# An SSD mixer whose small matmuls get a fixed order, with a projection unit between them, and weight low parts made by an accumulating DMA

## The chip, the cores and the metric

The kernel runs on one NeuronCore of a Trainium2 chip. The metric is the device time of one execution in microseconds (us). A core has the engines PE (TensorE, the matrix engine), DVE (VectorE), ACT (ScalarE), POOL (GpSimd) and SP (SyncE, which here only issues DMAs); each works through its own instructions in their fixed order and waits on semaphores for the others. DMAs are issued by SP, ACT or POOL and run beside the engines.

## What is computed

One inference step of a two-layer trunk for 512 prompt tokens and 8 x 8 sample tokens, 576 columns in all. Each layer is a half-step SwiGLU FFN, a mixer and another half-step FFN, with RMSNorm ahead of each. The mixer of layer 0, the one that matters here, is a Mamba-2 SSD mixer:

```python
def ssd_mixer(h, ssm0, conv0, w_in, conv_w, conv_b, dt_bias, a_log, d_skip, norm_g, w_out):
    proj = h @ w_in                                   # 1024 -> 2048 (z) + 4096 (x, B, C) + 32 (dt)
    z, xbc, dt_raw = jnp.split(proj, [D_INNER, D_INNER + CONV_DIM], axis=-1)
    xbc, conv_new = causal_dwconv(xbc, conv0, conv_w, conv_b)
    xs, Bm, Cm = jnp.split(jax.nn.silu(xbc), [D_INNER, D_INNER + SSD_GROUPS * D_STATE], axis=-1)
    dt = jax.nn.softplus((dt_raw + dt_bias).astype(f32))
    y, ssm_new = ssd_scan(xs, dt, A, Bm, Cm, ssm0)    # chunks of 128, 32 heads of 64, 8 groups, 128 states
    y = (y + d_skip * xs).reshape(bsz, l, D_INNER) * jax.nn.silu(z)
    ...                                               # RMSNorm within each of the 8 groups
    return y @ w_out, ssm_new, conv_new
```

Inside a chunk the scan multiplies a masked decay matrix exp(a_l - a_s) by C·B and applies it to x·dt; the states at the chunks' ends are chained, read out through C, and returned. All matrices are float32.

## The kernel before, in words

The activations lie transposed, 128 channels on the partitions and the 576 tokens along the row. A float32 product is made of three passes with rounded operands: weights and activations are split into a high part (a rounded copy) and a low part (the rest), and high·high, high·low and low·high are added up. A **unit** is one output tile of 128 channels: 8 blocks of 128 rows, three passes, two halves of 288 tokens, 48 matmuls of 128x288 (L339, in `passes`). Its weights come by one SP load of 512 KB into one of two `raw` buffers; `block` cuts them in two, writes the high part on ACT (L317) and the low part by a subtraction (L318), on POOL in this stage, into one of six `wb` buffers (two a unit). An output projection unit (`outproj`) has 2 or 4 blocks, so 12 or 24 matmuls.

The SSD stage has 48 units of w_in: 16 tiles of x (ct 0 to 15), 8 of B (16 to 23), 8 of C (24 to 31), 16 of z. `conv_in` runs a unit of x, B or C and the convolution behind it: three products with the norm's scale into `ext` (L637 to L639), ACT's first tap into `cacc` (L645) and three DVE taps (L647). The state of the convolution is loaded and transposed ahead of that, as four `crow` tiles of eight transposes each (L654, L657), through one buffer.

The 32 heads form 8 groups g of 4 heads, and each group two pairs j of two heads; p = 2g + j counts pairs. `group` makes, from B and C of a group, B with tokens on the partitions (`bnat`), C·B (`cbs`) and a block form of the sample tokens' B (`bblk`). `pair` does the scan of two heads: it transposes the old states (`nat` to `h0t`) and x, forms x·dt (`xdt`) and x·decay (`xw`, `xs`, `xd`), loads the decay sums `m` by SP (L800), masks them on POOL (L808 to L810), takes exponentials on ACT (L813), multiplies by `cbs` on DVE (L814, L815), and runs the small matmuls for states (L851), read-out (L864), the diagonal part (L871, L873) and the state update (L840). `spread` and four transposes prepare the decay numbers of all heads once. `gnorm` norms a group when its successor runs (`rnat`, L184, and `rbcast`, L218).

PSUM has eight banks: two `acc2` tiles of two banks in this stage (a unit's output each), and four `misc` banks for all small results.

The order of the instructions on each engine comes from the framework's scheduler, which lists them by a simulated time line (`TileContext(nc, schedule_with_timeline_sim=True)`) unless two of them were named by `tc.keep_in_program_order`, which then stay in the order of the code. Before, only the read-out and diagonal products of a pair are named so:

```python
for n, c in enumerate((3, 2, 1)):
    t = PE.matmul(out=pu[:, (c - 1) * P:c * P], lhsT=ht[:, c - 1], rhs=ctl[:, c * P:(c + 1) * P], start=True, stop=True)
    if n:
        pin(t)
```

All other small matmuls fall where the scheduler puts them, between the big ones of the units.

Of the kernel before, what the change touches and what calls it, by code (L numbers as in the profile page):

```python
# [8 lines left out]
F32 = mybir.dt.float32  # L9
# [40 lines left out]
def trunk(ctx, tc, x_prompt, x_sample, state_ssm, state_conv, state_pool,  # L50
# [127 lines left out]
    def rnat(accs, width):  # L178
        pt = misc()
        for c, (t0, n) in enumerate(BLOCKS):  # L180
            for h in range(0, P, 64):
                for i, acc in enumerate(accs):
                    t = t0 + h % n
                    PE.matmul(out=pt[h:h + 64, c:c + 1], lhsT=acc[:, t:t + 64], rhs=ones[:, 0:1], start=i == 0, stop=i == len(accs) - 1)  # L184
        return rstd(pt[:, 0:5], width)
# [28 lines left out]
    def rbcast(r):  # L214
        pt, pt2 = misc(), misc()
        for c, (t0, n) in enumerate(BLOCKS):
            o = pt[:, t0:t0 + n] if c < 4 else pt2[:, 0:n]
            PE.transpose(out=o, in_=r[0:n, c:c + 1].broadcast_to([n, P]), identity=ident[0:n, 0:n])  # L218
# [92 lines left out]
    def block(src, eng=None, pool=None):  # L311
# [6 lines left out]
        (eng or V).tensor_tensor(out=lo, in0=src, in1=hi.bitcast(F32), op=ALU.subtract)  # L318
# [15 lines left out]
    def passes(pd, w, acts, first, last):  # L334
        for h in range(2):
            n = 0
            for (wh, wl), (ah, al) in zip(w, acts):
                for lt, a in ((wh, ah), (wh, al), (wl, ah)):
                    PE.matmul(out=pd[:, h, 0:HALF], lhsT=lt, rhs=a[:, h * HALF:(h + 1) * HALF],  # L339
                              start=first and n == 0, stop=last and n == 3 * len(acts) - 1)  # L340
                    n += 1

    def mm(pt, w, acts):
        kn = len(acts)
        for k in range(0, kn, 4):
            passes(pt, w[k:k + 4], acts[k:k + 4], k == 0, k + 4 >= kn)
# [240 lines left out]
    def ssd(tail):  # L587
# [5 lines left out]
        with ExitStack() as st:  # L593
# [31 lines left out]

            def proj(c0, w=None):
                pt = acc_tile()
                mm(pt, w or unit(win[:, :, c0:c0 + P], G), hs)
                return pt

            def conv_in(ct):
# [4 lines left out]
                V.tensor_copy(out=es[:, :, 0:3], in_=cst[:, ct].rearrange("p (b e) -> p b e", e=3))  # L636
# [5 lines left out]
                V.tensor_copy(out=tails[:, ct, 3:27].rearrange("p (b e) -> p b e", e=3), in_=es[:, :, XST - 3:XST])  # L642
                a = wk.tile([P, XW], F32, name="cacc")
                n = XS0 + NB * XST - 3
                S.activation(out=a[:, 0:n], in_=ext[:, 0:n], func=AF.Identity, scale=cw[:, ct:ct + 1], bias=col("cb", ct))  # L645
                for k in range(1, 4):
                    V.scalar_tensor_tensor(out=a[:, 0:n], in0=ext[:, k:k + n], scalar=cw[:, k * 32 + ct:k * 32 + ct + 1], in1=a[:, 0:n],  # L647
                                           op0=ALU.mult, op1=ALU.add)
                return a
# [51 lines left out]
            pre = {}  # L701
            for ct in (16, 24):
                pre[ct] = conv_in(ct)
# [41 lines left out]
            V.tensor_scalar(out=mh[0:32], in0=mh[0:32], scalar1=hv[0:32, 2:3], scalar2=None, op0=ALU.mult)  # L745
            def spread():
                pt = misc()
                self_ = sel.rearrange("h a b -> h (a b)")
                PE.matmul(out=pt[:, 0:P], lhsT=self_, rhs=rhs.rearrange("h a b -> h (a b)"), start=True, stop=True)
# [21 lines left out]
            pin = tc.keep_in_program_order  # L771

            def stack(pt, src):
                s3 = wk.tile([P, 2, 3, 32], F32, name="s3", bufs=1)
                S.copy(out=s3, in_=src[:, SEQ:T].rearrange("p (q s) -> p q s", q=2).unsqueeze(2).broadcast_to([P, 2, 3, 32]))
                for q in range(2):
                    PE.transpose(out=pt[0:96, q * P:(q + 1) * P], in_=s3[:, q].rearrange("p a s -> p (a s)"), identity=ident)

            def pair(g, j, bt, ctl, bnat, bblk, cbs, xst, yt):
# [5 lines left out]
                h0t = wk.tile([P, NB, P], F32, name="h0t", bufs=1)  # L785
                for q in range(2):
                    pt = misc()
                    for i in range(4):
                        PE.transpose(out=pt[:, i * P:(i + 1) * P], in_=nat[:, 4 * q + i], identity=ident)
                    (V.tensor_copy if q else S.copy)(out=h0t[:, 4 * q:4 * q + 4], in_=pt.rearrange("p (b n) -> p b n", n=P))  # L790
                pq = misc()
                for b in range(NB):
                    r = b % 4 * 32
                    o = SEQ + b // 4 * 32
                    PE.matmul(out=pq[r:r + 32, (2 + b // 4) * P:(3 + b // 4) * P], lhsT=ctl[:, o:o + 32], rhs=h0t[:, b], start=True, stop=True)
                ch = wk.tile([P, 2, P], F32, name="ch", bufs=1)
# [423 lines left out]
```

## Time and profile before

| | us |
|---|---|
| median of three runs | 2357.1 (2356.55 to 2357.26) |
| the profiled execution: its time | 2357.4 |
| the profiled execution: span from first to last instruction | 2355.6 |
| PE busy | 2282.7 (97%) |
| DVE busy | 1874.8 (80%) |
| ACT busy | 1053.1 (45%) |
| POOL busy | 1030.7 (44%) |
| mean granted clock of PE | 0.987 |

PE has two clock levels, 1.2 and 2.4 GHz; the granted clock of a stretch is given as a share of the higher one. The SSD stage lies between about 423 and 1005 us; ahead of it and behind it are FFNs, which the change leaves as they are. A busy PE is not PE at its peak, since matmuls overlap and their ends are modelled: a rate is better read from the distance between the starts. Numbers in round brackets with an x are counts of instructions, in square brackets stands the time that an engine was idle just before, and what ended it.

### The profile page before, as it was taken

To read this page: it belongs to the slowest core of one execution; us is meant where nothing else is said; L and a number is where in the kernel's file an instruction comes from. 1 tells how busy PE (TensorE), PEld (TensorE's weight loads), DVE (VectorE), ACT (ScalarE), POOL (GpSimd) and SP (SyncE) were. 2 spreads that over 40 slices of the span, in tenths; PEclk is the share of its full clock that TensorE was granted. 3 is DMA by queue.
4 is the path that set the end of the run, shared out by engine and by line. 5 is a ranking of instruction groups with operands and counts; after the bars stand their busy time and mean duration, and the time that the engine had idled before them with its cause. 6 is when DMAs were issued, how large, how long until landed. Compare 5 with 4: busy or idle time off the path is not lost.

```text
span 2355.6 us, 43789 instructions
## 1 busy us (share of the span) xinstructions
PE 2282.7 (97%) x17572; PEld 2241.3 (95%) x17572; DVE 1874.8 (80%) x2950; ACT 1053.1 (45%) x1947; POOL 1030.7 (44%) x796
## 2 busy tenths in 40 slices
PE   8999999999999999989999999999999999999998
PEld 7999999988999999979999999999999899999997
DVE  8987778688887786798877799778876859778876
ACT  6444434455554545354444354334444344344433
POOL 4555440344444444155554535555531325555530
PEclk9999999999999999999999999999999999999999
DMA  5223222243443334412232232323222242322221
GB/s 150 90 90 108 81 90 66 62 138 110 134 135 107 118 110 113 116 57 88 90 108 82 89 99 72 108 64 99 90 81 67 67 117 83 108 68 94 90 73 59
DMA packets 272904, 222.23 MB, mean 94 GB/s; under 512 B 8322, under 2 KB 269042, under 8 KB 272701
## 3 DMA queue, kind: packets, MB, share of 16 engines
q1 hardware_dynamic: 269172, 218.04, 30.4%
q8 instruction: 139, 2.28, 0.4%
q10 hardware_dynamic: 3528, 1.39, 0.2%
q14 instruction: 65, 0.52, 0.1%
HBM read 206.46 MB, written 12.94 MB: 93 GB/s over the span
## 4 chain that ended last, share of the span: by engine, by line
PE 60%; DVE 9%; ACT 1%; DMA 1%; issue 1%; DVEq 0%; SPq 0%; ACTq 0%
PE acc L375 29%; PE acc L339 27%; DVE wh L256 1%; PE acc L554 1%; DVE cacc L647 1%; PE acc L479 1%; DVE ws L1102 1%; DVE m L814 0%; DMA rd<-in_pool_w_out 0%; PE misc L871 0%; DVE wb L318 0%; PE misc L851 0%; PE misc L864 0%; DVE glo L256 0%; ACT m L813 0%
## 5 line engine op out<-in xcount | busy, mean ns | idle before, releaser
L375 PE MATMUL acc<-wh,wb 128*128 128x288 f32 x6888 | 920.4, 295 | 4.2 <-DVE fo L380 2.3
L375 PEld LDWEIGHTS acc<-wh,wb 128*128 128x128 f32 x6888 | 916.1, 189 | 5.9 <-ACT wb L317 3.2
L339 PE MATMUL acc<-ghi,wb 128*128 128x288 f32 x2752 | 550.7, 295 | 0.3 <-DVE x L416 0.3
L339 PEld LDWEIGHTS acc<-ghi,wb 128*128 128x128 f32 x2752 | 441.2, 188 | 0.6 <-DVE x L416 0.5
L317 ACT CAST wb<-raw 128x512 fp32r<-128x512 f32 (+1 forms) x440 | 265.7, 607 | 358.8 <-PE acc L339 151.9
L339 PE MATMUL acc<-glo,wb 128*128 128x288 f32 x1376 | 404.2, 295 | 0.0
L339 PE MATMUL acc<-hhi,wb 128*128 128x288 f32 x1824 | 382.8, 300 | 2.3 <-DVE x L414 0.8
L318 POOL TENSOR_TENSOR wb<-raw,wb 128x512 fp32r<-128x512 f32 (+1 forms) x154 | 211.3, 1374 | 339.5 <-ACT wb L317 330.5
L318 DVE TENSOR_TENSOR wb<-ws,wb 128x512 fp32r<-128x512 f32 x328 | 325.8, 1004 | 15.0 <-ACT wb L317 14.9
L318 DVE TENSOR_TENSOR wb<-raw,wb 128x512 fp32r<-128x512 f32 (+1 forms) x286 | 269.3, 956 | 63.8 <-ACT wb L317 63.3
L317 ACT CAST wb<-ws 128x512 fp32r<-128x512 f32 x328 | 202.5, 621 | 241.0 <-PE acc L375 216.8
L339 PEld LDWEIGHTS acc<-hhi,wb 128*128 128x128 f32 x1824 | 297.8, 190 | 5.7 <-issue 1.6
L416 DVE SCALAR_TENSOR_TENSOR x<-acc,x 128x576 f32<-128x576 f32 x160 | 120.6, 754 | 194.8 <-PE acc L339 194.6
L339 PE MATMUL acc<-hlo,wb 128*128 128x288 f32 x912 | 273.4, 300 | 0.0
L356 POOL TENSOR_TENSOR ws<-raw,ws 128x512 f32<-128x512 f32 x82 | 151.9, 1852 | 246.0 <-DVE wb L318 241.0
L339 PEld LDWEIGHTS acc<-glo,wb 128*128 128x128 f32 x1376 | 257.9, 188 | 0.0
L318 POOL TENSOR_TENSOR wb<-rd,wb 128x512 fp32r<-128x512 f32 x128 | 174.8, 1374 | 184.0 <-ACT wb L317 183.8
L317 ACT CAST wb<-rd 128x512 fp32r<-128x512 f32 x196 | 114.0, 592 | 250.1 <-PE acc L339 219.3
L355 POOL TENSOR_TENSOR ws<-raw 128x512 f32<-128x512 f32 x82 | 124.6, 1520 | 160.4 <-DVE wb L318 160.4
L339 PEld LDWEIGHTS acc<-hlo,wb 128*128 128x128 f32 x912 | 173.0, 190 | 0.8 <-issue 0.2
L353 POOL TENSOR_TENSOR ws<-raw 128x512 f32<-128x512 f32 x82 | 128.4, 1566 | 87.5 <-DMA raw<-in_ffn_w_gate 78.4
L354 POOL TENSOR_TENSOR ws<-ws,raw 128x512 f32<-128x512 f32 x82 | 130.3, 1589 | 7.7 <-DVE wb L318 1.5
(329 smaller groups left out, 2897.5 us busy)
## 6 DMA issues: line engine op xcount, KB each, us to landing
raw<-in_ffn_w_gate SPq DMA_DIRECT2D x41, 1024.0 KB
raw<-in_ffn_w_up SPq DMA_DIRECT2D x41, 1024.0 KB
rd<-in_ffn_w_down SPq DMA_DIRECT2D x80, 512.0 KB
raw<-in_ssd_w_in SPq DMA_DIRECT2D x48, 512.0 KB
m<-ad SPq DMA_DIRECT2D x16, 576.0 KB
nat<-in_state_ssm SPq DMA_DIRECT2D x16, 512.0 KB
out<-nat SPq DMA_DIRECT2D x16, 512.0 KB
raw<-in_ssd_w_out SPq DMA_DIRECT2D x24, 256.0 KB
```

Source lines behind the costliest of these rows:

```text
L256: V.scalar_tensor_tensor(out=o, in0=xs, scalar=g, in1=sub, op0=ALU.mult, op1=ALU.subtract)
L317: S.copy(out=hi, in_=src)
L318: (eng or V).tensor_tensor(out=lo, in0=src, in1=hi.bitcast(F32), op=ALU.subtract)
L339: PE.matmul(out=pd[:, h, 0:HALF], lhsT=lt, rhs=a[:, h * HALF:(h + 1) * HALF], start=first and n == 0, stop=last and n == 3 * len(acts) - 1)
L353: G.tensor_tensor(out=s[0], in0=blk[2], in1=blk[3], op=ALU.add)
L354: G.tensor_tensor(out=s[1], in0=s[0], in1=blk[0], op=ALU.subtract)
L355: G.tensor_tensor(out=s[2], in0=blk[2], in1=blk[0], op=ALU.subtract)
L356: G.tensor_tensor(out=s[3], in0=blk[1], in1=s[1], op=ALU.subtract)
L375: PE.matmul(out=pt[:, m, 0:HALF], lhsT=wb[:, j, k], rhs=hh[k, h][:, slot], start=n == 0, stop=n == 11)
L416: V.scalar_tensor_tensor(out=halves(x[:, d]), in0=pt[:, :, 0:HALF], scalar=scale, in1=halves(x[:, d]), op0=ALU.mult, op1=ALU.add)
L479: PE.matmul(out=pd[:, m, 0:HALF], lhsT=w[:, a, 2 * k + m], rhs=b[:, h * HALF:(h + 1) * HALF], start=n == 0, stop=n == 5)
L554: PE.matmul(out=pt[:, m, 0:HALF], lhsT=wb[:, a, k], rhs=hh[k, b][:, slot], start=q == 0 and k == a == b == 0, stop=q == 1 and k == 3 and a ...
```

## The change

Four things change, all in the SSD stage.

**The low parts.** Where POOL subtracted, ACT now writes the negated high part into the low half (L323), and POOL issues a DMA that adds the raw weights to it (L324). PE waits for that DMA. The first two conv units keep the old form, their weights being split earlier.

**The order.** All small matmuls of the stage and the first big one of each unit are named for program order. `pair` becomes a generator that gives up control three times: loads; group A (transposes of the old states and of x); group B (C times old states, chunk states, state update); group C (read-out, diagonal part). In front of A of a first pair stands `group`, behind C of a first pair the norm of the last group. Between any two of them the loop puts a unit: conv 17+g or 25+g before A, conv p+1 between A and B, z between B and C, with four output projection units ahead of z in even groups.

**Where things are done.** Several small copies go from DVE to ACT, the two `m` products become one, `conv_in` is cut into the unit with its scaling and the `taps`, `bnat` and `cbs` come out of one `acc2` tile, the old states out of another, and `cbs` has one buffer for all groups.

**The end.** The first four of the last eight output projection units move up into the last pair.

```diff
-        (eng or V).tensor_tensor(out=lo, in0=src, in1=hi.bitcast(F32), op=ALU.subtract)
+        if eng == "dma":
+            S.activation(out=lo, in_=hi.bitcast(F32), func=AF.Identity, scale=-1.0)
+            G.dma_start(out=lo.bitcast(F32), in_=src, accum_op=ALU.add)
+        else:
+            (eng or V).tensor_tensor(out=lo, in0=src, in1=hi.bitcast(F32), op=ALU.subtract)
...
+                    if held and first and h == n == 0:
+                        tc.keep_in_program_order(t)
...
+                ph, pt, pt2 = acc_tile(), misc(), misc()
+                for b in range(NB):
+                    pin(PE.transpose(out=ph[:, b // 4, b % 4 * P:(b % 4 + 1) * P], in_=nat[:, b], identity=ident))
+                for c, (t0, n) in enumerate(BLOCKS):
+                    o = pt[0:n, c * P:(c + 1) * P] if c < 4 else pt2[0:n, 0:P]
+                    pin(PE.transpose(out=o, in_=xst[:, t0:t0 + n], identity=ident))
+                stack(pt2[:, P:512], xst)
...
+                V.tensor_tensor(out=m, in0=m, in1=cbs.unsqueeze(1).broadcast_to([P, 2, T]), op=ALU.mult)
...
+                pa, pt2 = acc_tile(), misc()
                 for c in range(4):
-                    PE.transpose(out=pt[:, c * P:(c + 1) * P], in_=bt[:, c * P:(c + 1) * P], identity=ident)
-                V.tensor_copy(out=bnat, in_=pt.rearrange("s (c n) -> s c n", n=P))
+                    pin(PE.transpose(out=pa[:, 0, c * P:(c + 1) * P], in_=bt[:, c * P:(c + 1) * P], identity=ident))
+                stack(pt2, bt)
+                for c in range(4):
+                    pin(PE.matmul(out=pa[:, 1, c * P:(c + 1) * P], lhsT=bt[:, c * P:(c + 1) * P], rhs=ctl[:, c * P:(c + 1) * P], start=True, stop=True))
...
+                S.copy(out=bnat, in_=pa[:, 0].rearrange("s (c n) -> s c n", n=P))
+                V.tensor_copy(out=cbs[:, 0:SEQ], in_=pa[:, 1])
...
+                for j in range(2):
+                    p = 2 * g + j
+                    if g < 7:
+                        conv_in((25 if j else 17) + g)
+                    elif j:
+                        zs = zproj(p)
+                    if j == 0:
...
+                        bnat, bblk = group(bt, ctl)
...
+                    work = pair(g, j, bt, ctl, bnat, bblk, x_, yt)
+                    next(work)
+                    if p == 0:
+                        spread()
+                    next(work)
+                    if g < 7 and j == 0:
+                        taps(17 + g)
+                        bc_.append(bt_ctl(g + 1, 0))
...
+                    if p < 15:
+                        conv_in(p + 1)
+                    else:
+                        outproj(10, 4, range(0, 2))
+                    if g and j == 0:
+                        r = rnat([sqacc], 256, True)
+                    next(work)
+                    if p < 15:
+                        taps(p + 1)
+                        x_ = xtile(p + 1)
                     if g % 2 == 0 and g:
                         outproj(max(2 * g - 6, 0), 4 if g > 2 else 2, range(4 * j, 4 * j + 4))
...
+                    if p < 15:
+                        zs = zproj(p)
+                    else:
+                        outproj(10, 4, range(2, 4))
+                    work.send(zs)
```

**What stands where.** PE at the start of the stage, before: the norm's broadcast (`rr`), a run of crow transposes among the big matmuls of the first unit (acc_4805).

```order
L339 MATMUL acc_4805<-hhi,wb 128x288 x2
L339 MATMUL acc_4805<-hlo,wb 128x288
L218 MATMUL misc<-ident,rr 128x128 x4
L218 MATMUL misc<-ident,rr 128x64
L657 MATMUL misc<-ident,crow 128x24 x8
L339 MATMUL acc_4805<-hhi,wb 128x288 x2
L339 MATMUL acc_4805<-hlo,wb 128x288
```

PE at the same place after, from the last matmuls of the dt projection (acc_4726) to the first of that unit:

```order
L347 MATMUL acc_4726<-hlo,wb 128x288
L347 MATMUL acc_4726<-hhi,wb 128x288
L220 MATMUL misc<-ident,rr 128x128 x4
L220 MATMUL misc<-ident,rr 128x64
L673 MATMUL misc<-ident,crow 128x24 x32
L683 MATMUL misc<-ident,vrow 128x3
L347 MATMUL acc_4805<-hhi,wb 128x288
```

The four runs of eight crow transposes, which lay 25 to 30 big matmuls apart, now stand in one run ahead of the unit.

PE where group 1 begins, before: `bnat`'s transposes (L925), the sample tokens' transposes (L777) and C·B (L936) inside one unit (acc_6105).

```order
L840 MATMUL misc<-bblk,xw_5587 128x512
L925 MATMUL misc<-ident,bt 128x128 x4
L339 MATMUL acc_6105<-hhi,wb 128x288 x2
L777 MATMUL misc<-ident,s_5723 96x128 x2
L339 MATMUL acc_6105<-hlo,wb 128x288
L339 MATMUL acc_6105<-hhi,wb 128x288 x2
L339 MATMUL acc_6105<-hlo,wb 128x288
L339 MATMUL acc_6105<-hhi,wb 128x288 x2
L936 MATMUL misc<-ctl,bt 128x128 x4
```

PE at the same place after, from the end of conv unit 18 (acc_5795) to the first matmul of conv unit 3 (acc_5957):

```order
L347 MATMUL acc_5795<-hhi,wb 128x288
L929 MATMUL acc_5868<-ident,bt 128x128 x4
L794 MATMUL misc<-ident,s_5874 96x128 x2
L932 MATMUL acc_5868<-ctl,bt 128x128 x4
L933 MATMUL misc<-ctl,bt 64x64
L811 MATMUL acc_5899<-ident,nat 128x128 x8
L814 MATMUL misc<-ident,xst 128x128 x4
L814 MATMUL misc<-ident,xst 64x128
L794 MATMUL misc<-ident,s_5915 96x128 x2
L347 MATMUL acc_5957<-hhi,wb 128x288
```

`group` and group A stand in one block between two units. acc_5868 (the tile `pa`) is the buffer that acc_5957 takes again, so the last row waits for the copies out of `pa`.

DVE at that place, before, around the copy of `cbs`:

```order
L843 SCALAR_TENSOR_TENSOR nat<-nat,decp,misc 128x128 x3
L926 COPY bnat<-misc 128x512 [waits PE_49]
L969 TENSOR_TENSOR zs<-acc_6026,rb 128x576 [waits DVE_49]
L949 TENSOR_TENSOR sqacc<-sqacc,sq 128x576 [waits Activation_49]
L937 COPY cbs<-misc 128x512 [waits PE_49]
L931 TENSOR_TENSOR bsp<-bns,bsp 32x256 [waits Activation_49]
```

DVE at that place after, from the scaling of unit 18 to the copies out of the two acc tiles:

```order
L649 TENSOR_TENSOR ext<-acc_5795,rb 128x288 [waits PE_49]
L650 TENSOR_TENSOR ext<-acc_5795,rb 128x224
L651 TENSOR_TENSOR ext<-acc_5795,rb 128x8x8
L825 TENSOR_TENSOR xw<-misc,anat 128x512 [waits PE_49]
L828 TENSOR_TENSOR xdt<-misc,anat 128x512
L826 TENSOR_TENSOR xs_5922<-misc,wsn 96x256 [waits PE_49]
L829 TENSOR_TENSOR xd_4653<-misc,anat 64x128
L664 SCALAR_TENSOR_TENSOR cacc<-ext,cw,cacc 128x600 [waits DVE_49,Activation_49,Pool_49]
L935 COPY cbs<-acc_5868 128x512 [waits Activation_49]
L824 COPY h0t<-acc_5899 128x512 [waits Activation_49]
```

The copy of `cbs`, which stood behind work of the pair before, now stands behind the products of the x transposes (L814) and a tap.

## Rows read from the trace of the kernel before

**Rows 1.** The page, part 1: busy us, share of the span, instructions, by engine.

```profile
PE 2282.7 (97%) x17572; PEld 2241.3 (95%) x17572; DVE 1874.8 (80%) x2950; ACT 1053.1 (45%) x1947; POOL 1030.7 (44%) x796
```

**Rows 2.** Windows, whole core: window, us, busy us (x instructions) of PE, PEld, DVE, ACT, POOL, clock, DMA share, GB/s.

```profile
480.00:530.00 50.00, 49.51 (x401) 46.41 (x402) 43.09 (x99) 30.02 (x72) 23.93 (x25) 0.93 0.47 138
...
680.00:730.00 50.00, 47.03 (x379) 44.85 (x378) 39.61 (x85) 26.36 (x55) 21.75 (x20) 0.93 0.37 105
...
830.00:880.00 50.00, 47.69 (x408) 45.77 (x407) 40.55 (x94) 21.41 (x46) 21.27 (x19) 1.00 0.39 113
...
930.00:980.00 50.00, 45.94 (x386) 42.17 (x383) 42.86 (x94) 18.05 (x35) 14.09 (x11) 0.97 0.38 106
```

**Rows 3.** Waits of PE, 423 to 1010: us in total, times, longest.

```profile
PE misc L795 <- DVE h0t L790: 5.1, 3, 2.5
PE misc L749 <- DVE rhs L744: 4.9, 1, 4.9
PE acc L339 <- DVE ext L639: 3.8, 2, 2.3
PE misc L184 <- DVE sqacc L949: 3.0, 1, 3.0
```

**Rows 4.** Timeline of PE: start, us, operation, in brackets the idle time before it.

```profile
477.77 0.58 PE L749 MATMUL misc<-rhs,sel 64*128 64x128 f32 x1 [4.91 <-DVE rhs L744]
```

**Rows 5.** Windows of PE alone: window, us, busy us, granted clock, DMA share, GB/s.

```profile
477.50:487.50 10.00, 9.33 (x47) 0.51 0.63 187
...
541.00:545.00 4.00, 3.86 (x25) 0.62 0.11 31
```

**Rows 6.** Timeline of PE at the end of a run of small matmuls.

```profile
603.96 0.38 PE L339 MATMUL acc<-hlo,wb 128*128 128x288 f32 x1
604.17 0.43 PE L339 MATMUL acc<-hhi,wb 128*128 128x288 f32 x2
604.44 0.29 PE L339 MATMUL acc<-hlo,wb 128*128 128x288 f32 x1
```

**Rows 7.** Timeline of SP's queue: the second and third crow load.

```profile
428.08 4.42 SPq L654 DMA_DIRECT2D crow<-in_state_conv  x2
```

**Rows 8.** Timeline of PE: the second and third run of crow transposes.

```profile
431.48 0.67 PE L657 MATMUL misc<-ident,crow 24*128 24x24 f32 x8
...
436.25 0.67 PE L657 MATMUL misc<-ident,crow 24*128 24x24 f32 x8
```

**Rows 9.** Lines of DVE by shape, 480 to 1010: busy us, mean ns, idle before and its releaser.

```profile
L647 DVE SCALAR_TENSOR_TENSOR cacc<-ext,cw,cacc 128x600 f32<-128x600 f32 x84 | 86.8, 1033 | 17.9 <-ACT cacc L645 9.4 <-POOL wb L318 7.5
L843 DVE SCALAR_TENSOR_TENSOR nat<-nat,decp,misc 128x128 f32<-128x128 f32 x128 | 35.7, 339 | 0.0
...
L827 DVE TENSOR_TENSOR xw<-misc,anat 128x512 f32<-128x512 f32 x16 | 10.8, 677 | 0.0
...
L832 DVE TENSOR_TENSOR xs<-misc,wsn 96x256 f32<-96x256 f32 x16 | 6.5, 405 | 0.0
...
L937 DVE COPY cbs<-misc 128x512 f32<-128x512 f32 x7 | 4.8, 680 | 0.0
...
L829 DVE TENSOR_TENSOR xd<-misc,anat 64x128 f32<-64x128 f32 x16 | 4.4, 272 | 0.0
```

**Rows 10.** Timeline of SP's queue: one load of m.

```profile
615.76 0.34 SPq L800 DMA_DIRECT2D m<-ad  x1
```

**Rows 11.** Timeline of POOL: the mask on that m.

```profile
620.93 1.09 POOL L808 TENSOR_SCALAR_AFFINE_SELECT m<-m 128x1024 f32<-128x1024 f32 x1 [1.04 <-DMA m<-ad]
```

**Rows 12.** Timeline of ACT: the first eight exponentials on it.

```profile
622.80 2.46 ACT L813 ACTIVATE m<-m,anat 128x128 f32<-128x128 f32 x8
```

**Rows 13.** Lines of ACT by shape, 480 to 1010.

```profile
L317 ACT CAST wb<-raw 128x512 fp32r<-128x512 f32 x108 | 66.5, 615 | 105.1 <-PE acc L339 101.0 <-DMA raw<-in_ssd_w_in 3.7
```

**Rows 14.** Lines of POOL by shape, 480 to 1010.

```profile
L318 POOL TENSOR_TENSOR wb<-raw,wb 128x512 fp32r<-128x512 f32 x104 | 149.9, 1444 | 213.7 <-ACT wb L317 207.2 <-issue 3.7 <-DMA raw<-in_ssd_w_out 2.8
```

More of the change, by code (lines that the diff above doesn't have):

```diff
@@ L183, in rnat @@
                     t = t0 + h % n
-                    PE.matmul(out=pt[h:h + 64, c:c + 1], lhsT=acc[:, t:t + 64], rhs=ones[:, 0:1], start=i == 0, stop=i == len(accs) - 1)
+                    k = PE.matmul(out=pt[h:h + 64, c:c + 1], lhsT=acc[:, t:t + 64], rhs=ones[:, 0:1], start=i == 0, stop=i == len(accs) - 1)
+                    if held:
+                        tc.keep_in_program_order(k)
         return rstd(pt[:, 0:5], width)
@@ L332, in unit, with passes @@
         return [(bl[k // 4][:, 0, k % 4], bl[k // 4][:, 1, k % 4]) for k in range(kn)]
-    def passes(pd, w, acts, first, last):
+    def passes(pd, w, acts, first, last, held=False):
         for h in range(2):
@@ L784, in pair @@
                 nc.sync.dma_start(out=nat, in_=sv)
[L785 to L796, printed above, removed]
-                V.tensor_copy(out=ch, in_=pq[:, 2 * P:4 * P].rearrange("p (q n) -> p q n", q=2))
                 m = wk.tile([P, 2, T], F32, name="m")
@@ L846, in pair @@
-                if pr == 15:
-                    update()
-                stp = misc()
-                for c in range(4):
-                    PE.matmul(out=stp[:, c * P:(c + 1) * P], lhsT=bnat[:, c], rhs=xw[:, c].rearrange("s h p -> s (h p)"), start=True, stop=True)
+                yield
+                pq, stp, pus = misc(), misc(), [misc(), misc()]
+                for b in range(NB):
+                    r = b % 4 * 32
+                    o = SEQ + b // 4 * 32
+                    pin(PE.matmul(out=pq[r:r + 32, (2 + b // 4) * P:(3 + b // 4) * P], lhsT=ctl[:, o:o + 32], rhs=h0t[:, b], start=True, stop=True))
@@ new lines, in pair @@
+                for c in range(4):
+                    pin(PE.matmul(out=stp[:, c * P:(c + 1) * P], lhsT=bnat[:, c], rhs=xw[:, c].rearrange("s h p -> s (h p)"), start=True, stop=True))
+                for q in range(2):
+                    pin(PE.matmul(out=pus[q], lhsT=xw3[:, q].rearrange("s h p -> s (h p)"), rhs=bblk[:, q].rearrange("s b n -> s (b n)"), start=True, stop=True))
+                ch = wk.tile([P, 2, P], F32, name="ch", bufs=1)
+                V.tensor_copy(out=ch, in_=pq[:, 2 * P:4 * P].rearrange("p (q n) -> p q n", q=2))
@@ L933, in group @@
                     G.tensor_tensor(out=bblk[:, q], in0=bsp[:, q:q + 1].broadcast_to([96, 4, P]), in1=bc(bmask, P), op=ALU.mult)
-                pt = misc()
-                for c in range(4):
-                    PE.matmul(out=pt[:, c * P:(c + 1) * P], lhsT=bt[:, c * P:(c + 1) * P], rhs=ctl[:, c * P:(c + 1) * P], start=True, stop=True)
-                V.tensor_copy(out=cbs[:, 0:SEQ], in_=pt)
-                pt = misc()
-                PE.matmul(out=pt[0:64, 0:64], lhsT=bt[:, SEQ:T], rhs=ctl[:, SEQ:T], start=True, stop=True)
-                S.copy(out=cbs[0:64, SEQ:T], in_=pt[0:64, 0:64])
-                return bnat, bblk, cbs
+                return bnat, bblk
             def gsum(ys, add=True):
@@ L946, in gsum @@
                 S.activation(out=sq, in_=ys[1], func=AF.Square)
[L947 to L950 removed]
+                if add:
+                    V.tensor_tensor(out=sqacc, in0=sqacc, in1=sq, op=ALU.add)
+                return [sqacc, sq]
             def gtile(g):
```

201 lines of the change are left out of this document (94 added, 107 removed).

## The prediction

> **What bounds the kernel now.** I read the page first: PE is busy for 97% of the span [rows 1] and makes most of the chain that ended last, so the time changes only where PE waits, runs at half clock or does more work. The change touches one stage, the SSD mixer, some 423 to 1005 us. There I read the table of windows for the granted clock [rows 2], then the list of what PE waited for [rows 3], then the longest wait itself and the clock behind it [rows 4, 5]. The reader should see three losses.
>
> Waits: the four largest are 5.1, 4.9, 3.8 and 3.0 us, nine smaller ones make 6.5, together 23.3 us [rows 3].
>
> Clock: after the wait of 4.91 us PE ran at 0.51, the 1.2 GHz level, for 10 us [rows 4, 5]; after one of 2.5 us (the longest of the three in the first row of [rows 3]) it ran part of four us so [rows 5]. Window by window, length times (1 minus clock) is 3.5, 3.5, 0 and 1.5 us [rows 2]; two more windows at 0.97, of 57 and 50 us, add 1.7 and 1.5: 11.7 us.
>
> Switching: in a run of one kind, matmuls of 128x288 start 0.133 us apart; the one that follows a run of small matmuls takes 0.21 (603.96 to 604.17) [rows 6]. The program has 136 such runs in the stage.
>
> So 23.3 + 11.7 = **35 us** are to be had from waits and clock, and something from switching. DVE has 43.1 of 50 us busy in one window [rows 2] but is nowhere the bound by itself.
>
> **What the change removes.** PE's order in the stage becomes fixed: 48 groups of small matmuls (three a pair, A, B, C) with a whole unit of 48 big ones between, so some 52 runs for 136. [...] I take **10**. If every old wait goes, the profiled execution's 2357.4 us (span 2355.6 and 1.8 around it, 0.3 over the median of the runs) becomes 2357.4 - 35 - 10 = 2312. Nothing else on PE is removed: the same matmuls are issued.
>
> Low parts: 124 blocks lose a POOL subtract of 1444 ns [rows 14] and gain an ACT negation, by the cast of the same shape 615 ns [rows 13], some 76 us of ACT in a stage where it is busy 18 to 30 us in 50 [rows 2], and an accumulating DMA. Cost on PE: nothing, if it lands in time. The slot of a block is given back three units before PE needs its new content, that is 3 x 48 x 0.133 = 19 us and the groups between, against 1.2 us on ACT, POOL's issue and the landing. Such a DMA is not in the trace; the nearest row is the load of m, 576 KB in 5.2 us [rows 10, 11], and the content is 256 KB. Bounds 2 to 6 us, both under the cover, so I take zero. Were the cover gone, each block would cost PE its excess over 3.2 us (24 matmuls).
>
> The Trainium skill ("DMA: Bandwidth & Descriptors", section "Anatomy of one DMA — SWDGE (gpsimd) path") has about 2.0 us and bytes over 436,000 per us for a DMA that GpSimd issues, an estimate of 2.6 us here. By it the sum would stay as it is; no run here shows the figure.
>
> DVE loses copies (two per conv tile, bnat, ht0, a second m product), which is no gain by itself, since it is not the bound.
>
> **What it adds.** A pinned PE can't fill a wait with other work, so each wait that the new order holds is paid in full. I followed the waits of the changed order to the instruction that ends each.
>
> (a) Prologue. The 32 crow transposes stand in one run, and the crow tile has one buffer, so three loads follow on the transposes of the one before, with nothing beside them. Before, 25 to 30 big matmuls lay between: the load was issued at 428.08 and its transposes ran at 431.48, the next at 436.25 [rows 7, 8]. 3.4 us is thus the upper bound of a round, 2 a low one (no shorter load is in sight): 3 x 2.5 = 7.5 us, 6 to 10. Of the clock after it: 2 (0 to 5, by the 5 us that the 10 us at half clock lost). SP's later loads queue behind these three; they have 20 us of slack.
>
> (b) In pair 0 the ACT cast of xw, for which group B waits, is queued behind more than 16 exponentials at 0.31 us [rows 12]: 3 us, 0 to 6.
>
> (c) **The group's first pair.** With two acc tiles, the group's B transposes and C·B products now take one (pa), and the next unit needs that one back. Its first matmul waits for the DVE copy cbs, and in the new DVE order cbs stands behind xw, xdt, xs, xd and a conv tap, all of which wait for the x transposes that end group A. DVE needs 0.68 + 0.68 + 0.41 + 0.27 + 1.03 + 0.68 = 3.75 us [rows 9], PE has 0.3 us of small matmuls left: 3.4 us, in g = 1, 3, 4, 5, 6. In g = 2 the tap comes first and waits for ACT: 4.5. In g = 0 the copy stands early, in g = 7 too. ACT hardly adds: m is loaded when C of the pair before ends, lands 5.2 us later [rows 10, 11], 1.1 for the mask [rows 11], 3.1 for ten exponentials [rows 12]: 9.4, when PE is 3 us into the group of 3.7; every us that m lands later is added. Sum 21.5; low end 6 x 2.5 (a tap without POOL beside it), high end 6 x 4.7. Queued behind cbs on DVE are h0t, the other taps and m, which B needs only 6.4 us later.
>
> (d) Clock after (c). The wait of 2.5 us cost (1 - 0.62) x 4 = 1.5 us of clock [rows 5], the one of 2.3 nothing, the one of 4.9 some 5. I take 1.5 for each of six: 9 us; 0 to 20.
>
> (e) In second pairs the next unit waits for ext, since DVE still has the norm of the last group (four products, two splits and the y steps, which I estimate at 8 us against the unit's 6.4, of which group A covers most of the excess): 0.5 x 7 = 3.5 us; 0 to 6.
>
> (f) From B to C in odd groups lie 6.4 us. DVE has ext, ch, eight nat updates at 0.34, three taps at 1.03 [rows 9] and six short ht steps in mixed order, by my estimate 7 us before the last ht: 0.4 x 9 = 3.5; 0 to 8.
>
> (g) In g = 2 the output projection has units of 12 matmuls, 1.6 us; its third waits for an add to x that stands behind B's DVE work: 3 in one pair, 1 in the other: 4; 2 to 7.
>
> (h) The end of the stage stays as it is, 1.5 of the old waits.
>
> Sum of (a) to (h): 9.5 + 3 + 21.5 + 9 + 3.5 + 3.5 + 4 + 1.5 = **55.5 us**; low ends 24.5, high ends 92.
>
> So 2312 + 55.5 = **2368 us**. The ends: 2357 - 35 - 15 + 25 = 2332, and 2357 - 35 - 7 + 90 = 2405. Break-even is at 45 us of new waits.
>
> **Rivals.**
>
> Faster: the waits come at their low ends. Place: the cbs copy. Without POOL's subtracts beside it DVE's tap goes below its 1.03 mean, m lands a little sooner, the wait stays near 2.5 us and the clock does not fall, as it didn't after the wait of 2.3 us for ext [rows 3], which lies in the window 830 to 880 at clock 1.00 [rows 2]. For it: every old loss goes for sure. Against: the order of DVE is fixed and its sum alone is over 3 us. It decides at some 2 us a pair, clock included. 2312 + 25 = 2337. Chance 0.28.
>
> No change that can be told: new waits of 40 to 50 us, 2352 to 2362. Within 0.2% is about what a measurement of this kernel can't tell from nothing. Chance 0.17.
>
> Slower by far: the low parts come late, so the DMA does not do what the POOL subtract did. It decides where one block takes over 3.2 us of throughput, from POOL's issue to the landing; at 3.5 us the 124 blocks cost PE 37 us, on top of my sum 2406. For it: the DMA share is already 0.37 to 0.47 in the stage [rows 2], and the raw buffer (two) is held until the DMA has landed. Against: 256 KB against 576 KB in 5.2 us. Chance 0.13.
>
> The Trainium skill (the same page, section "SWDGE vs HWDGE vs iDMA") speaks for this rival: GpSimd writes the descriptors of such a DMA into SBUF, and DVE can lock it out there. By that rule an issue would be late while DVE is busy; no trace here shows such an issue.
>
> **How the numbers follow.** My forecast, a little slower by the waits of the fixed order, 2362 to 2390: 0.42. It is the likeliest, so 2368 stands. Below 2332 and above 2405 I leave less than 2 in 10. Faster 0.28, same 0.17, slower 0.42 + 0.13 = 0.55.
>
> **What would show it.** In the profile after: the longest wait of PE in the stage named by cbs, six times, 2.5 to 5 us; crow transposes with idle time of 2 to 3.4 us before each of three runs; clock rows below 1.00 once a group; no wait of PE on the DMA of wb; the h0t, rhs and sqacc waits gone; ACT busy about two thirds of the stage. If PE waits for wb, the last rival is right; if the cbs rows add up to less than 12 us with the clock at 1.00 throughout, the first. It would be wrong from the start if the old waits came back under other names, or if a low part landed in more than 15 us.

## The result and the profile after

The changed kernel takes **2432.3 us** (median of four, 2430.8 to 2436.7), the kernel before 2357.2 beside it: a ratio of 1.0316 (95% interval 1.0302 to 1.0329). The forecast was 2368 with a range up to 2405: slower was right, but 75 us came where 11 had been forecast. The lines of the page that answer to [rows 1], and the DMA queues:

```profile
span 2431.9 us, 44121 instructions
PE 2300.4 (95%) x17572; PEld 2260.6 (93%) x17572; DVE 1804.1 (74%) x2847; ACT 1133.5 (47%) x2161; POOL 960.9 (40%) x796
...
q1 hardware_dynamic: 269172, 218.04, 29.4%
q0 software_dynamic: 17856, 31.47, 7.8%
...
PE 68%; DVE 14%; DMA 9%; ACT 4%; issue 4%; POOL 0%; SPq 0%; ACTq 0%; DVEq 0%; POOLq 0%
```

By engine, the chain that ended last was this in the kernel before:

```profile
PE 60%; DVE 9%; ACT 1%; DMA 1%; issue 1%; DVEq 0%; SPq 0%; ACTq 0%
```

ACT is busy 80 us longer and PE 18, DVE and POOL 71 and 70 us less, so no engine has become the bound by its work. But DMA now makes 9% of the chain that ended last, after 1%. The windows of [rows 2] again, then four of 5 us (columns: busy us and instructions of PE, PEld, DVE, ACT, POOL; granted clock, DMA share, GB/s):

```profile
480.00:530.00 50.00, 42.35 (x337) 40.14 (x330) 30.70 (x75) 36.33 (x88) 12.53 (x19) 0.93 0.71 157
680.00:730.00 50.00, 42.87 (x346) 41.18 (x345) 31.82 (x73) 33.91 (x79) 14.41 (x19) 0.93 0.68 161
830.00:880.00 50.00, 45.36 (x382) 43.48 (x381) 31.33 (x71) 26.62 (x59) 13.52 (x17) 0.97 0.67 153
930.00:980.00 50.00, 47.46 (x405) 46.16 (x403) 28.05 (x76) 28.74 (x63) 12.37 (x17) 1.00 0.67 151
...
535.00:540.00 5.00, 1.25 (x12) 0.98 (x10) 1.29 (x2) 3.92 (x11) 2.61 (x4) 0.97 0.67 193
540.00:545.00 5.00, 1.84 (x7) 1.42 (x8) 3.01 (x6) 4.50 (x14) 0.86 (x1) 0.50 0.22 38
545.00:550.00 5.00, 5.00 (x23) 5.00 (x23) 4.91 (x5) 0.01 (x1) 2.87 (x2) 0.50 0.61 132
550.00:555.00 5.00, 5.00 (x65) 4.63 (x65) 2.95 (x10) 4.94 (x11) 1.08 (x3) 1.00 0.09 25
```

PE stands still for most of 535 to 545 and runs at 0.50, the 1.2 GHz level, until 550. What it, ACT and SP waited for (us in total, times, longest; PE from 423 to 1100, the others from 480 to 1080), to lay beside [rows 3]:

```profile
PE misc L794 <- ACT s L792: 26.0, 6, 6.1
PE acc L347 <- DVE cbs L935: 14.0, 6, 3.6
PE misc L673 <- DMA crow<-in_state_conv: 9.8, 3, 5.1
PE misc L852 <- DVE xw L831: 8.7, 4, 5.9
PE acc L347 <- DVE x L424: 8.3, 5, 2.2
...
ACT wb L321 <- DMA raw<-in_ssd_w_out: 54.1, 17, 7.0
ACT wb L321 <- DMA raw<-in_ssd_w_in: 39.8, 11, 7.3
ACT L841 <- DMA m<-ad: 19.5, 9, 4.9
...
SPq L333 <- DMA wb<-raw: 405.9, 70, 15.1
```

The largest row, 26.0 us, was put at nothing in the forecast: PE waits in all six first pairs of g = 1 to 6 for `s`, ACT's small copy of x's sample columns in `stack`. This is how one of them comes about (ACT's time line, with idle time and what ended it in brackets; one row each of SP, POOL and PE behind it):

```profile
531.27 0.62 ACT L321 CAST wb<-raw 128x512 fp32r<-128x512 f32 x1 [1.38 <-DMA raw<-in_ssd_w_in]
531.92 0.63 ACT L323 ACTIVATE wb<-wb 128x512 fp32r<-128x512 f32 x1
536.07 1.28 ACT L841 ACT_TABLE_LOAD   x1 [3.52 <-DMA m<-ad]
537.37 2.92 ACT L841 ACTIVATE m<-m,anat 128x128 f32<-128x128 f32 x10
540.19 0.60 ACT L321 CAST wb<-raw 128x512 fp32r<-128x512 f32 x1
540.70 0.35 ACT L792 COPY s<-xst 128x192 f32<-128x192 f32 x1
...
527.09 2.26 SPq L803 DMA_DIRECT2D m<-ad  x1
...
536.13 1.09 POOL L836 TENSOR_SCALAR_AFFINE_SELECT m<-m 128x1024 f32<-128x1024 f32 x1 [8.31 <-DMA m<-ad]
...
541.10 0.66 PE L794 MATMUL misc<-ident,s 128*96 128x128 f32 x2 [4.85 <-ACT s L792]
```

`s` needs 0.35 us and its input was there. But ACT works its queue in order, and ahead of `s` the scheduler has put the ten exponentials of the **next** pair. They wait for that pair's m, which landed 9.0 us after its issue (527.09 to 536.1). A cast that waited for raw stands ahead of them.

### The profile page after: what moved, and what is told of

It reads as the page before. It is cut to its first block, busy times and chain, and to the rows that moved or that the text cites. A ratio compares the mean times of both kernels' runs of the same rounds, so it can differ in the third digit from the quotient of the medians.

```text
span 2431.9 us, 44121 instructions
## 1 busy us (share of the span) xinstructions
PE 2300.4 (95%) x17572; PEld 2260.6 (93%) x17572; DVE 1804.1 (74%) x2847; ACT 1133.5 (47%) x2161; POOL 960.9 (40%) x796
## 4 chain that ended last, share of the span: by engine, by line
PE 68%; DVE 14%; DMA 9%; ACT 4%; issue 4%; POOL 0%; SPq 0%; ACTq 0%; DVEq 0%; POOLq 0%
PE acc L385 33%; PE acc L347 31%; DVE wb L326 3%; DMA m<-ad 3%; DMA wb<-raw 2%; PE acc L564 1%; DMA raw<-in_ssd_w_in 1%; DVE wh L260 1%; ACT m L841 1%; PE acc L489 1%; ACT wb L321 1%; DVE fo L390 1%; DVE cacc L664 1%; DMA out<-nat 1%; DVE fo L393 1%
## 5 line engine op out<-in xcount | busy, mean ns | idle before, releaser
L347 PE MATMUL acc<-hhi,wb 128*128 128x288 f32 x1824 | 390.9, 306 | 15.0 <-DVE cbs L935 14.0
L347 PEld LDWEIGHTS acc<-hhi,wb 128*128 128x128 f32 x1824 | 309.2, 197 | 19.3 <-DVE cbs L935 16.6
L324 POOL DMA_DIRECT2D wb<-raw x124 | 107.9, 877 | 337.8 <-ACT wb L323 234.6
L347 PEld LDWEIGHTS acc<-hlo,wb 128*128 128x128 f32 x912 | 179.6, 197 | 0.4
```

The source lines that it names most:

```text
L324: G.dma_start(out=lo.bitcast(F32), in_=src, accum_op=ALU.add)
L347: t = PE.matmul(out=pd[:, h, 0:HALF], lhsT=lt, rhs=a[:, h * HALF:(h + 1) * HALF], start=first and n == 0, stop=last and n == 3 * len(acts) ...
```

## The experiments

Theory D: the accumulating DMAs are the cause, through ACT; they hold the raw buffers, so that casts wait, and fill the DMA engines, so that m is late. Theory P: it is the fixed order of PE by itself. Theory A: it is the load that the negations put on ACT. Medians in us; "ratio" is to the kernel before on the same chip. The runs come from several chips, on which the kernel before took 2357.2 to 2360.5, so a difference of under some 3 us between two rows is read from the ratios.

| run | what differs | us | ratio (95%) |
|---|---|---|---|
| e1_pool_low | after, low parts by POOL | 2389.6 | 1.0120 (1.0094 to 1.0146) |
| e2_unpinned_dma | before, low parts by DMA | 2379.1 | 1.0085 (1.0066 to 1.0103) |
| e3_raw4 | after, ring of four raw halves | 2406.7 | 1.0197 (1.0181 to 1.0213) |
| e4_no_dma | after, DMA left out | 2375.3 | 1.0065 (1.0050 to 1.0080) |
| e5_exps_own_pair | e1, exponentials behind own pair | 2359.7 | 1.0001 (0.9991 to 1.0010) |
| e6_cbs_first | e1, cbs first on DVE | 2380.2 | 1.0091 (1.0076 to 1.0106) |
| e7_crow_once | e1, conv state in one tile | 2381.0 | 1.0090 (1.0073 to 1.0107) |
| e8_all_three | e5, e6, e7 together | 2352.2 | 0.9970 (0.9957 to 0.9983) |
| e9_after_exps | after, exponentials as e5 | 2415.3 | 1.0234 (1.0213 to 1.0255) |
| e10_after_exps_raw4 | e9 and the ring of e3 | 2356.9 | 0.9990 (0.9981 to 1.0000) |
| e11_decb_on_sp | e8, decb's load on SP | 2349.4 | 0.9959 (0.9944 to 0.9974) |
| e12_plain_dma | after, plain DMAs | 2396.4 | 1.0157 (1.0139 to 1.0174) |
| e13_dma_all_edits | e10 and the edits of e11 | **2341.4** | 0.9923 (0.9908 to 0.9938) |
| e14_before_prologue | before, e7's and e11's prologue | 2364.0 | 1.0023 (1.0014 to 1.0033) |
| e15_pool_all_edits_raw4 | e13, low parts by POOL | 2349.4 | 0.9961 (0.9947 to 0.9975) |

### One part of the change at a time (e1 to e4)

e1: `"dma"` becomes `G` in `proj` and `outproj`. e2: the `"dma"` branch of `block` and its two calls in the kernel before. e4: the `G.dma_start` line of `block` is left out, so the low part stays at minus the high part. e3:

```diff
     def unit(src, eng=None):
         kn = src.shape[1]
-        v = load(src, src.shape[1:])
+        if eng == "dma":
+            if not ring:
+                for _ in range(2):
+                    rw = raw.tile([P, 2048], F32, name="raw")
+                    ring.extend((rw[:, 0:1024], rw[:, 1024:2048]))
+            ring.append(ring.pop(0))
+            v = ring[-1][:, 0:kn * P].rearrange("p (k f) -> p k f", f=P)
+            nc.sync.dma_start(out=v, in_=src)
...
```

> The changed kernel with the low parts of the SSD projections made by POOL's subtract again, as before the change; PE's fixed order stays. Theory D (the accumulating DMAs make the loss: they hold both raw buffers until they land and fill the DMA engines, so ACT stands at casts and exponentials and PE waits for its copies): 2355 to 2375 us, the waits of PE on the copy s (26.0 us in the changed kernel) fall below 8, those of SP's projection loads on wb go away. Theory P (the fixed order alone makes the loss): 2420 to 2435, the waits on s stay near 26. Theory A (the negations on ACT, some 70 us of its time, make the loss): 2355 to 2375 too; the fourth run of this call tells it from D.

> The kernel before with the low parts by ACT negation and accumulating DMA, and nothing else of the change: PE's order stays free. Theory D: slower than before by 15 to 60 us (2372 to 2417), since raw buffers and DMA engines are as in the changed kernel, but a free order fills part of the waits; the DMA share of the stage goes to 0.6 or more, and SP's projection loads wait for wb's DMA by 200 us or more. Theory P: 2350 to 2362, as before. Theory A: 2365 to 2385.

> The changed kernel with the projections' raw loads in a ring of four half tiles (a raw tile of 8 KB per partition is only half used by a load of 512 KB), so that a load need not wait for the accumulating DMA of two units before. Theory D has two halves. If holding the buffers is the larger: 2380 to 2405, SP's waits of 406 us on wb's DMA fall below 120, ACT's waits of 94 us on raw loads below 30. If the time on the DMA engines is the larger: 2420 to 2440, m still lands 6 us or more after its issue and ACT and POOL still wait for it by 20 and 75 us. Theories P and A: 2425 to 2440, nothing that PE waits for changes.

> The changed kernel without the accumulating DMA: the negations on ACT stay, the low part is left at minus the high part, so the raw content is not added to it. Theory D: 2350 to 2375, within 10 us of the first run of this call. Theory A: 2415 to 2435, as with the DMA. Theory P: 2420 to 2435, as with the DMA.

The change without its DMAs costs 30 us (e1: 2389.6 against 2359.9 for the kernel before on that chip), the DMAs alone 19 (e2), both 75. So D and P each hold a part, neither as large as expected, and 26 us belong to the two together. I call the 30 us those of the fixed order, but e1 also holds the copies moved to ACT and the shared acc tiles, and no run undid these by themselves. A is out: with the negations and no DMA it is 2375.3, not 2415. (D had e4 within 10 us of e1; it is 14 faster.) In e2 SP's loads wait 339.7 us for wb's DMA, as D said, but a free PE loses little by it.

e3 gave 25 us, between the two halves of D. The casts' waits for raw (94 us) are gone, but SP still waits 356 us for wb's DMA, where under 120 had been expected: with four buffers a load waits for the DMA of the fourth load before it, not of the second, and no cast of the stage's weights waits for it. And the exponentials took the casts' place (SP, ACT, PE):

```profile
SPq L347 <- DMA wb<-raw: 356.2, 67, 13.8
...
ACT L852 <- DMA m<-ad: 49.4, 13, 7.9
...
PE misc L805 <- ACT s L803: 29.7, 7, 7.8
```

### The waits of the fixed order (e5 to e8)

In e1, with no DMA of the low parts, PE still waits for `s` and then for `cbs`. Its two rows in the list of waits, then the rows around the same place, PE, ACT, DVE and POOL:

```profile
PE acc L347 <- DVE cbs L935: 17.1, 6, 3.3
PE misc L794 <- ACT s L792: 10.1, 6, 2.7
...
534.73 0.42 PE L794 MATMUL misc<-ident,s 128*96 128x128 f32 x2 [2.51 <-ACT s L792]
538.47 0.61 PE L347 MATMUL acc<-hhi,wb 128*128 128x288 f32 x1 [3.31 <-DVE cbs L935]
...
531.00 2.92 ACT L841 ACTIVATE m<-m,anat 128x128 f32<-128x128 f32 x10
...
534.33 0.35 ACT L792 COPY s<-xst 128x192 f32<-128x192 f32 x1
...
534.80 0.88 ACT L657 ACTIVATE cacc<-ext,cols,cw 128x600 f32<-128x600 f32 x1
...
535.77 0.84 DVE L664 SCALAR_TENSOR_TENSOR cacc<-ext,cw,cacc 128x600 f32<-128x600 f32 x1 [6.00 <-POOL wb L326]
...
531.07 1.26 POOL L326 TENSOR_TENSOR wb<-raw,wb 128x512 fp32r<-128x512 f32 x1
```

DVE stood idle for 6.00 us before a tap, with `cbs` behind it. The row names POOL's wb, but that had ended at 532.3; what ended at 535.68, right ahead of the tap, is ACT's `cacc` (534.80 + 0.88), and that stood behind the exponentials too. At this place both waits have one root. The edits, e5, e6 and e7 in turn:

```diff
-                        S.activation(out=m[0:n, h2, t0:t0 + n], in_=m[0:n, h2, t0:t0 + n], func=AF.Exp, bias=anat[0:n, c, 0, h0 + h2:h0 + h2 + 1])
+                        pin(S.activation(out=m[0:n, h2, t0:t0 + n], in_=m[0:n, h2, t0:t0 + n], func=AF.Exp, bias=anat[0:n, c, 0, h0 + h2:h0 + h2 + 1]))
...
-                V.tensor_copy(out=cbs[:, 0:SEQ], in_=pa[:, 1])
+                cc = V.tensor_copy(out=cbs[:, 0:SEQ], in_=pa[:, 1])
...
-                    next(work)
+                    if j == 0:
+                        with tc.issue_after(cc.ins):
+                            next(work)
+                    else:
+                        next(work)
...
-            for q in range(4):
-                crow = dp.tile([27, 2, 512], F32, name="crow")
...
+            crow = dp.tile([P, 2, 512], F32, name="crow")
...
+            for q in range(4):
+                nc.sync.dma_start(out=cf[32 * q:32 * q + 24], in_=state_conv[0].rearrange("b t c -> (b t) c")[:, q * 1024:(q + 1) * 1024])
+            for a in range(2):
+                pt = misc()
+                for i in range(4):
+                    PE.transpose(out=pt[:, i * P:(i + 1) * P], in_=crow[:, a, i * P:(i + 1) * P], identity=ident)
...
```

> The first run of the study (fixed order, low parts by POOL) with the ten exponentials of a pair held behind the cast of xw of the same pair on ACT, so that the exponentials of the next pair, which wait for that pair's m, no longer stand ahead of this pair's copy s. Theory Q (ACT's queue order makes those waits): PE's waits on s, 10.1 us in that run, fall below 2, clock loss falls by some 5, so 2389.6 becomes 2368 to 2382. Rival (the copy is late because ACT is too busy, whatever its order): the waits on s stay above 7, 2385 to 2395; or the product m is late for group C and PE waits there instead, 2385 to 2400.

> The first run of the study with DVE's operations of a group's first pair queued behind the copy cbs, which hands back the acc tile that the next unit needs. Theory of the prediction (the copy is late since it stands behind xw, xdt and a tap on DVE): PE's waits named cbs, 17.1 us in six, fall below 4; with 5 to 10 of clock, 2389.6 becomes 2362 to 2374. Rival (the copy is late since DVE is still busy with work before group A): the waits stay above 10, 2382 to 2392; or xw and h0t are late for group B instead, 2380 to 2392.

> The first run of the study with the conv state loaded into one tile of 128 partitions by four loads in a row and transposed by eight full transposes in place of 32 (the three rounds of load and transposes in the prologue go). If the rounds are worth what they showed (7.0 us of waits, and about 10 of the 12 us that the clock of 0.79 cost in 423 to 480): 2370 to 2378, clock of 423 to 480 above 0.92. If the clock falls there for another reason (too few matmuls ahead of the stage): 2380 to 2384.

> The three edits of this call together. If the waits of PE add as they do one by one: 34 us of waits and 15 to 25 of clock go, 2389.6 becomes 2332 to 2345, faster than before the change (2357 to 2360). If a fixed order only moves the wait to the next late operand: 2360 to 2380, with new names (h0t, xw, ht or ext) holding 10 us or more.

Holding the exponentials behind their own pair gave 30 us, more than Q had: as much as the fixed order had cost. The waits on `s` are gone from the list and `cbs` fell with them, untouched by the edit itself:

```profile
PE acc L347 <- DVE cbs L935: 9.9, 6, 2.0
```

e6 shows the same from the other side: with `cbs` first on DVE its waits stayed at 14.4, since the tap ahead of it still waited for ACT, and the 9 us it gave came in part from `s` (10.1 to 5.9). The prediction's reason for that wait, the work queued on DVE, was the smaller one: 2.7 us by e6 against 7.2 by e5, and 7.3 us of `cbs` are left with both edits (e8), which no run followed up. e7 gave 8.5, less than the rounds had shown: the crow waits went and one of 8.5 on the first x came, with the clock of 423 to 480 at 0.88 after 0.79. Together they beat the kernel before by 0.3%, but missed the 2332 to 2345 of full addition: a wait of 9.3 on that x was left.

### Both causes in the changed kernel (e9 to e12)

e9 and e10 put e5's edit on the changed kernel, without and with the ring. e11: `nc.scalar` becomes `nc.sync` at the load of decb. e12: `accum_op=ALU.add` is dropped, so the raw weights overwrite the low half and are not added to it.

> The changed kernel, its accumulating DMAs included, with the exponentials held behind the cast of xw of their own pair, as in the fifth run of the study. If the order of ACT's queue is worth the same with the DMAs as with POOL's subtract (30 us): 2395 to 2408. If most of the DMAs' cost of 43 us also came through that place (m landing later while the exponentials stand ahead of the copy s): 2360 to 2385. If ACT's casts, which wait for raw loads by 94 us, are the place instead: 2405 to 2430, with PE's waits on s still above 12 us.

> The same with the ring of four half tiles for the raw loads (third run of the study), so neither of the two places is left: the exponentials are out of the way and the raw loads are early. If these two are all that the DMAs cost: 2350 to 2370, as the fifth run (2359.7). If the DMA engines' time is a cost by itself (m lands late for group C, or nat for group A): 2375 to 2405, with PE waits named ht, m or nat in the trace.

> The eighth run of the study (all three edits, 2352.2 us) with the broadcast load of the decay (decb) moved from ACT's DMA queue to SP's. In that run ACT stood 5.7 us at this load in the prologue, and behind it stands the silu of the first x, for which PE waited 9.3 us. If that is the place: the wait falls to 2 to 5 us, 2342 to 2348. If the first x is late because of DVE's taps (two took 4.95 us there): the wait stays above 7, 2349 to 2355.

> The changed kernel with plain DMAs in place of the accumulating ones: the raw content overwrites the negated high part and is not added to it; the same bytes, queues and waits stay. If the adding is what costs the DMA engines (29.37 MB took 29.5% of the 16 engines in 480 to 1080, 60.39 MB of the hardware queue 34.8%): the software queue's share of the span falls from 7.8% to 3.5 to 5%, a block lands in under 3.5 us, and the kernel takes 2395 to 2420. If it is the path by GpSimd's queue, whatever it does: 7 to 8% and 2425 to 2440.

From the changed kernel at 2432.3 the ring alone takes 25.6 us, the order of the exponentials alone 17.0, both **75.4**, all that the change lost. They are two stops in one queue: with one gone ACT stands at the other, and `s` and `cacc` stand behind either. e9 is the third case of its expectation, the casts, though the waits on `s` came to 10.2 where over 12 had been expected. ACT's waits and PE's in e9:

```profile
ACT wb L321 <- DMA raw<-in_ssd_w_out: 62.0, 18, 5.4
ACT wb L321 <- DMA raw<-in_ssd_w_in: 50.6, 15, 5.7
...
PE acc L347 <- DVE cbs L935: 17.0, 6, 3.8
PE misc L794 <- ACT s L792: 10.2, 4, 3.5
```

In e10 no such row of ACT is left, and PE's two:

```profile
PE acc L358 <- DVE cbs L946: 9.3, 6, 1.7
...
PE misc L805 <- ACT s L803: 1.2, 1, 1.2
```

m still lands late in e10 (behind the first two pairs, POOL's mask began 5.3 to 8.9 us after the issue, 3.6 to 6.2 in the kernel before), but nothing urgent stands behind it. e11 took the wait on the first x from 9.3 to 5.4 us, between its two cases, so ACT's stop at decb was part of that wait; the rest was not followed further. Its time, 2349.4 for 2352.2, lies in the second case, and the two ratios (0.9970 and 0.9959) do not tell it from no gain. e12 belongs to the hardware below.

### What is left of the change (e13 to e15)

> The tenth run of the study (the changed kernel with its accumulating DMAs, exponentials behind their own pair, ring of four raw half tiles; 2356.9 us) with the edits of the eleventh as well: cbs first on DVE, the conv state in one tile, decb on SP. If the DMAs cost nothing more: 2345 to 2351, as the eleventh run (2349.4). If their load on the DMA engines still delays m or nat: 2353 to 2360, with PE waits by those names.

> The kernel before with the prologue's two edits alone (conv state in one tile with eight transposes, decb on SP), its free order as it was. If the eleventh run's gain of 10 us is that of the fixed order: 2355 to 2362, no change, since the old order had its big matmuls between the transposes. If it is the prologue's: 2346 to 2352.

> The thirteenth run (2341.4 us) with the low parts by POOL's subtract in place of negation and accumulating DMA; ring of four and all other edits as there. If the DMAs are the gain (POOL's subtracts of 1.4 us on a port that they share with DVE, DVE's 1.03 us taps): 2346 to 2352. If the earlier raw loads are: 2338 to 2344.

With every edit the changed kernel takes 2341.4 us, 0.8% under the kernel before and faster than either case of e13, and 8 us under the same with POOL's subtract (e15, inside the case that the DMAs are the gain): once nothing queues behind them the accumulating DMAs are a gain. It lies in less waiting and less clock loss, 28.3 and 8.5 us in the stage of e13 against 30.8 and 13.5 in e15; why these are less is only partly seen. The Trainium skill ("SBUF — State Buffer", section "Who interferes with whom") says that a DVE instruction with two inputs in SBUF contends with a GpSimd instruction that reads SBUF; the traces agree in sign, DVE's taps take 1003 ns in the mean with the subtracts and 960 without, but 80 taps of 43 ns are 3.5 us of DVE and do not prove the 8. e14 says that the prologue's edits do not help the old order: they cost it 0.2%, a little more than its case of no change allowed. The gain of e13 is thus not that of these edits by themselves; they pay only in the fixed order.

## Why the prediction was right or wrong

Sums over the stage: all rows of PE's list of waits from 423 to 1130 us, and length times (1 minus clock) of the 50 us windows from 423 to 1123.

| | before | after | e1 | e5 | e10 | e13 |
|---|---|---|---|---|---|---|
| waits | 33.9 | 93.4 | 56.1 | 38.0 | 37.7 | 28.3 |
| clock | 16.5 | 45.5 | 35.5 | 22.0 | 17.5 | 8.5 |

The span grew by 76 us, waits by 59.5 and clock losses by 29. I put the 12 too much down to what fewer switches gave back and to time that counts twice, when PE waits at the low clock; no run parts the two.

**What goes.** Right: the waits on h0t (5.1 to 1.2), rhs and sqacc are gone. The switching gain of 10 is not contradicted, nor is it shown: the span less all its waits and clock losses, over the whole run, is 2261 us before and 2251 in e1, e5 and e10, but 2240 in the changed kernel and 2259 in e11, and 2257 in e14 with the old order. Of the 7 and 15 in the ends of the range, 84 runs fewer at the 0.08 us of [rows 6] give the 7; no run shows the 15. In the kernel before, transposes of one kind (L789) start 0.109 us apart in runs of up to eight small matmuls and 0.110 in longer ones.

**(c), the step that failed first.** The place was right (the first pairs of g = 1 to 6), the sum was not. "ACT hardly adds" was 5.2 + 1.1 + 3.1 = 9.4 us from the end of C to the end of the exponentials. e1 shows what was left out (the last products of C, the issue of m, the mask on it):

```profile
522.00 0.28 PE L882 MATMUL misc<-m,xd 128*64 128x64 f32 x4
...
523.73 0.57 SPq L803 DMA_DIRECT2D m<-ad  x1
...
529.76 1.09 POOL L836 TENSOR_SCALAR_AFFINE_SELECT m<-m 128x1024 f32<-128x1024 f32 x1 [5.65 <-DMA m<-ad]
```

C ended at 522.3; m was issued at 523.73, behind nat's load; POOL's mask began at 529.76, 6.0 later, beside nat and raw on the DMA engines; the table load came before the exponentials, which ended at 533.9; and a cast stood ahead of `s` at 534.33: 12 us. In the changed kernel it is 14.4 (526.3 to 540.70). Each row of the forecast's chain was taken from the kernel before, where the loads do not come together: m went out at 615.76 and the next load 4 us later, while in e1 nat, m and raw go out from 523.31 to 524.41. And what stands behind the exponentials on ACT was not followed: `s` was put at nothing, and the conv's `cacc`, and through it the tap ahead of `cbs`, came in for g = 2 alone. Waits of 40 us (26.0 + 14.0) stand where 21.5 had been put.

**(d), clock.** 29 us more where the forecast had some 11 come and 11.7 go. The price per wait was that of a wait of 2.5 us; at the place shown PE stood 5 us on `s` and 2 more on `cbs` a moment later, and after that ran at 0.50 until 550, like the 4.91 us wait of [rows 4].

**The low parts, the step that took the time out of the range.** "Cost on PE: nothing, if it lands in time" failed although its condition held: 256 KB land in 4.1 us in the median, inside the bounds of 2 to 6, and PE never waited for wb's DMA. Still the DMA in place of POOL's subtract cost 43 us in the fixed order (2432.3 less 2389.6); without it e1 lies inside the range. The prediction had seen that raw is held until the DMA has landed and that the DMA share was 0.37 to 0.47, but priced both by PE's throughput, at 3.2 us a block. What stops is ACT, whose casts wait for raw, and PE waits for that in another place; e3, e9 and e10 show it. The question "who queues behind the waiting instruction" was asked for DVE's `cbs`, not for ACT's cast.

**The rest.** (a) 9.8 us for 7.5 (6 to 10), though one round of 5.1 us lay above the bound of 3.4; e7 is worth 8.5. (b) 5.9 us at 487 for 3 (0 to 6). (e) and (f) came to 0 and 0.6 for 3.5 each. (g) right in kind: of 8.3 us on x some 2.8 lie in g = 2. New and not forecast: 7.8 us for ACT's fin; the longest of these waits, 3.3 us at 641, ends when fin gets its turn behind casts that waited for raw. The Trainium skill's rule in the prediction that DVE can lock GpSimd out of its descriptors ("DMA: Bandwidth & Descriptors", section "SWDGE vs HWDGE vs iDMA") was not tried by any run here. The rival "slower by far" (2406, chance 0.13) had the right suspect and the wrong path: it wanted PE to be short of blocks. That slower won is thus in part luck: the waits of the fixed order, on which the forecast stood, came to less than half of the loss. Of the signs named, `cbs` six times came (2.1 to 3.6 us), though it was not the longest wait, and so did the crow rounds; ACT was busy for 56% of 423 to 1080, where two thirds were forecast.

## What to carry to other kernels

When the order of one engine is fixed, list for each small result that it waits for what stands ahead of that result in its producer's queue, and whether any of it waits for a DMA of later work: here, in e1, moving ten exponentials of the next pair from ahead of a 0.35 us copy gave back 30 us. A new reader of a load buffer delayed the next load here, and ACT, which consumes the loads in order, passed this on to everything behind it. Two such stops in one queue hid part of each other (25.6 and 17.0 us alone, 75.4 together), so undo them together before judging either.

## What the runs showed of the hardware

The addition is what makes these DMAs dear. Accumulating (the changed kernel) and plain (e12), queue (packets, MB, share of 16 engines) and landing:

```profile
q0 software_dynamic: 17856, 31.47, 7.8%
...
wb<-raw POOLq DMA_DIRECT2D x116, 256.0 KB, 4.1
```

```profile
q0 software_dynamic: 9664, 31.47, 3.5%
...
wb<-raw POOLq DMA_DIRECT2D x116, 256.0 KB, 3.0
```

With the addition the same bytes take 2.2 times the engines' time and nearly twice the packets, and POOL's issue takes 877 ns for 544. Plain, the changed kernel took 2396.4 us: of the DMAs' cost 36 us hung on the addition. The Trainium skill ("DMA: Bandwidth & Descriptors", section "Anatomy of one DMA — SWDGE (gpsimd) path") has 2.0 us and bytes over 436,000 per us, an estimate of 2.6 us here, near the 3.0 of the plain ones; the 4.1 of the accumulating ones is above it.

The issue of one and the same DMA did not always take the same time: from the third load of m on, SP's issue took 0.34 to 0.36 us in the kernel before and up to 2.26 in the changed kernel, there behind 5 us with a DMA share of 0.94. That the busy DMA engines made it long is not shown.
